# One split of x instead of three: an input projection in three sweeps, with the recurrences beside two of them

## The chip, the cores and the metric

The kernel runs on one core of one Trainium2 chip. A core has a matrix engine (PE; its weight loads are listed apart as PEld), a vector engine (DVE), a scalar engine (ACT), a general engine (POOL) and a sync engine (SP), which here does nothing but issue DMAs. The metric is the device time of one execution in microseconds; smaller is better. Three runs of the kernel before gave 3016.13, 3017.36 and 3020.99 us. All durations and waits are from one profiled execution of it.

## The reference

One encoder block on x of 2048 rows by 1024 columns, float32. The part that the change touches:

```python
h = rmsnorm(x, norm1_g)
p = h @ w_in                          # 1024 -> 1536: lru_x 512 | lru_gate 512 | fourier 512
c = centred_depthwise_conv(lru_x)     # width 4, along positions
h_f = rglru(c, ..., reverse=False)    # gates: 8 heads of 64x64 matmuls, sigmoid, then a linear
h_b = rglru(c, ..., reverse=True)     #   recurrence along the 2048 positions, in each direction
y_lru  = gelu(lru_gate) * (h_f + h_b)
y_four = real(fft2(fourier columns))  # per group of 128 channels
x = x + concat([y_lru, y_four]) @ w_out
x = x + expert_choice_moe(rmsnorm(x)) # 16 SwiGLU experts, 256 rows each
out = rmsnorm_final(x)
```

## The kernel before

**Matmuls.** Each float32 product is three matmuls in a reduced float32 format (`mm3`, L78 to L80): high part times high part, and the two mixed products. To have the parts, `split` copies a tile with rounding on ACT (the high part, L85 or with a row factor L88) and subtracts on DVE (the low part, L86 or L89). So whatever PE reads has first been through one ACT and one DVE (or POOL) instruction.

**Order.** The kernel is written in Tile, whose scheduler sets the order on each engine within dependencies; `soon()` raises the priority of what stands in it, and `tc.issue_after` holds an instruction behind another. Each engine then runs its instructions strictly in that order. Nearly all loads are issued from SP, also in one order: a DMA whose condition isn't met holds up all that stand behind it. POOL issues a few stores itself. A DMA also waits for one of eight lanes per kind of queue to be free (`DMAHW0` to `DMAHW7` in the lists below).

**Stages up to w_out**, all in `pre_moe`. Blocks are 128 columns; a chunk is 256 rows of x, a tile 128 rows.

- *First sweep*, `p1(0)`: columns of lru_x, blocks 0 and 1: 8 chunks of 48 matmuls of 256 columns. x comes as `xr` tiles of 128x512 and is split to `xx` (L197 ACT, L201 DVE or L199 POOL). The squares of x (L204, ACT) are added on POOL (`xa`, L239); `rms` sums them over the partitions by matmuls with a column of ones (L286), which gives one number per row, spread over partitions. Since the projection has rows along the free axis, `rstd` is stored to a buffer `r_d` in HBM and loaded back into all partitions as `R` (L222, SP). The evacuation (L254, DVE) multiplies the product by R into `u`.
- *Second sweep*, `p1(1)`: blocks 2 and 3, x loaded and split again; ahead of it stands `lru(0)`, the convolution (L328 POOL, L330 DVE), the split of its result c (`ch` L331, `cl` L332), the gates' matmuls (`gt<-ch,gm`, 48 of 512 columns), their sigmoids (L339), tanh, exp, square root, and two scans (L361, L363, DVE) of block 0.
- *Fourier sweep*: 16 tiles, 27 matmuls of 512 columns each (`mixin`, `stage1`), x loaded and split a third time (`load_xt`: L212 DVE, L213 POOL). `lru(1)`, `lru(2)` and `lru(3)` stand among the tiles. The first FFT stage's results `v` go to `v_d` in HBM by stores from POOL.
- *Gate sweep*: 8 chunks of 96 matmuls of 256 columns, x loaded and split a fourth time; per chunk DVE multiplies by R (`tm`, L435), ACT takes the Gelu (L438), DVE multiplies into `u` (L441).
- *FFT*: the second stage over positions and the channel stage, from `v_d` (`vraw`) and twiddles (`traw`); w_out is loaded and split meanwhile (`woraw`, L458 ACT, L459 POOL).
- *w_out*, routing and the experts follow.

Of the kernel before, what the change touches and what calls it, by code (L numbers as in the profile page):

```python
# [75 lines left out]
def mm3(nc, out, sh, sl, mh, ml, first=True, last=True, shared=False):  # L76
    """shared: groups of one bank are interleaved; the bank's first matmul alone starts it"""
    nc.tensor.matmul(out, sh, mh, start=first, stop=False, skip_group_check=shared)  # L78
    nc.tensor.matmul(out, sh, ml, start=False, stop=False, skip_group_check=shared)  # L79
    return nc.tensor.matmul(out, sl, mh, start=False, stop=last, skip_group_check=shared)  # L80
# [67 lines left out]
def pre_moe(tc, nc, a, g, ctx):  # L148
# [11 lines left out]
    last = {}  # L160

    for n, b in (("wraw", 2), ("w", 8), ("xraw", 4), ("xx", 6)):
        WP.tile([P, 512 * (1 + (n in ("w", "xx")))], F32R, name=n, bufs=b)

    def load_w(c0, n, k):
# [7 lines left out]
    def load_w2(c0, k2):
        """two k of a 256-column part"""
        with soon():
            if c0:
                raw = WP.tile([P, 2, 256], F32, name="wraw", bufs=2)
            else:
                raw = pr.tile([P, 2, 256], F32, name="wr1", bufs=8)
            nc.sync.dma_start(raw, a["w_u"][c0 // 256, k2])  # L180
            if c0:
                w = pl.tile([P, 2, 2, 256], F32R, name="fv"[k2 // 2], bufs=2)
            else:
                w = pr.tile([P, 2, 2, 256], F32R, name="w1", bufs=4)
            for i in range(2):
                split(nc, raw[:, i], w[:, 0, i], w[:, 1, i], g.g1[:, 2 * k2 + i:2 * k2 + i + 1])
        return [w[:, :, 0], w[:, :, 1]]

    def load_x(c, k2, pool=False, sq=None):
        with soon():  # L190
            if sq is not None:
                raw = pr.tile([P, 2, 256], F32, name="xr1", bufs=8)
            else:
                raw = WP.tile([P, 2, 256], F32, name="xraw", bufs=4)
            x = WP.tile([P, 2, 2, 256], F32R, name="xx", bufs=6)
            nc.sync.dma_start(raw, a["xT"][c, k2])
            last["ACT"] = nc.scalar.copy(x[:, 0], raw)  # L197
            if pool:
                GP.tensor_tensor(x[:, 1], raw, x[:, 0].bitcast(F32), OP.subtract)  # L199
            else:  # L200
                last["DVE"] = V.tensor_tensor(x[:, 1], raw, x[:, 0].bitcast(F32), OP.subtract)  # L201
# [4 lines left out]

    def load_xt(t, hf):
        with soon():
            raw = WP.tile([P, 4, P], F32, name="xraw", bufs=4)
# [2 lines left out]
            V.tensor_copy(x[:, 0], raw)  # L212
            GP.tensor_tensor(x[:, 1], raw, x[:, 0].bitcast(F32), OP.subtract)  # L213
# [5 lines left out]
    def load_R(c):  # L219
        R = WP.tile([P, 256], F32, name="R", bufs=2)  # L220
        src = g.r_d[c:c + 1]
        nc.sync.dma_start(R, bass.AP(tensor=src.tensor, offset=src.offset, ap=[[0, P], [1, 256]]))  # L222
        return R

    qbi = lambda x: x.rearrange("p (q b i) -> p q b i", q=2, b=16)

    def p1_load(h, c, w):
        xx = []
        acc = pr.tile([P, 2, 256], F32, name="xa", bufs=4) if h == 0 else None
        for k2 in range(4):  # L230
            if c == 0:
                w[2 * k2], w[2 * k2 + 1] = load_w2(256 * h, k2)
            if h:
                xx += load_x(c, k2, pool=k2 % 2 == 1)
                continue
            sq = pr.tile([P, 2, 256], F32, name="sq0", bufs=8) if k2 else acc
            xx += load_x(c, k2, sq=sq)
# [8 lines left out]

    def p1(h, w, pre):
        pend = []

        def evac(c, pt):  # L250
            R = load_R(c)
            with soon():
                for b in range(2):
                    V.tensor_tensor(u_view(2 * h + b, c), qbi(pt[:, b * 256:(b + 1) * 256]), qbi(R), OP.mult)  # L254
# [1001 lines left out]
```

## Time and profile before

| | |
|---|---|
| median of 3 runs | 3017.36 us (3016.13 to 3020.99) |
| span of the profiled execution | 3013.5 us, granted PE clock 0.969 |
| PE, weight loads, DVE, ACT, POOL busy in it | 2835.5, 2611.9, 1859.7, 1300.4, 559.6 us |
| first sweep | 0 to 95.3 us |
| second sweep | 95.3 to 180.6 us |
| fourier sweep | 180.6 to 371 us |
| gate sweep | 371 to 464 us |
| FFT | 464 to 517 us |
| w_out, the second norm, the router | 517 to 759 us |
| choice of rows, experts, final norm | 759 to 3013.5 us |

The profiled execution's span lies 3.9 us below the median of the runs; what surrounds it isn't in the profile. The stages' limits are read from the timeline of PE. In the profile a row of a group gives line, engine, operation, output and inputs with their shapes, the count, then busy us and mean ns of one, and behind the bar the idle time of the engine before them with what ended it. "PEclk" is the share of full clock granted to PE.

### The profile page before, as it was taken

Reading aid. Unit: us, or ns where it says so; the run is one execution under the profiler, and the core shown is the slowest. Engines: PE = TensorE matmul, PEld = TensorE weight load, DVE = VectorE, ACT = ScalarE, POOL = GpSimd, SP = SyncE. Lnnn points to the kernel's source line nnn. Section 1 sums busy time; section 2 is a strip of 40 time slices with the busy share of each in tenths; the row PEclk is TensorE's granted clock in tenths of the full one; section 3 lists DMA queues with packets and bytes.
Section 4 is the critical chain, followed back from the end, with each engine's and each line's share of the span. In section 5 each row is a group of like instructions: output and inputs, shape, how many; then the busy total and the mean of one; then the engine's idle time right before and its main releaser. Section 6 shows DMA issues by size and latency. Waiting matters only on the chain.

```text
span 3013.5 us, 45335 instructions
## 1 busy us (share of the span) xinstructions
PE 2835.5 (94%) x19199; PEld 2611.9 (87%) x19199; DVE 1859.7 (62%) x2146; ACT 1300.4 (43%) x1377; POOL 559.6 (19%) x412
## 2 busy tenths in 40 slices
PE   6677898996789999999999999999999999999997
PEld 6666697775679999999999999999999999999997
DVE  6588877556876555555665555555555655555565
ACT  5455654333234434343443444443434444343465
POOL 4375402002322111112021111111020111111110
PEclk8888999998889999999999999999999999999999
DMA  5532243454346565656656565656566565656585
GB/s 158 121 109 67 89 151 108 150 159 175 140 166 212 196 196 196 198 197 207 201 188 213 196 199 197 205 194 202 192 196 206 198 209 196 198 196 197 196 296 205
DMA packets 129196, 548.07 MB, mean 182 GB/s; under 512 B 20416, under 2 KB 37216, under 8 KB 79840
## 3 DMA queue, kind: packets, MB, share of 16 engines
q1 hardware_dynamic: 107664, 481.16, 47.3%
q0 software_dynamic: 19008, 63.98, 7.5%
q8 instruction: 150, 2.46, 0.3%
q14 instruction: 54, 0.44, 0.0%
q10 hardware_dynamic: 2320, 0.04, 0.0%
HBM read 498.97 MB, written 46.15 MB: 181 GB/s over the span
## 4 chain that ended last, share of the span: by engine, by line
PE 69%; DVE 3%; issue 2%; DMA 1%; POOL 0%; POOLq 0%; ACT 0%; DVEq 0%
PE mm L78 16%; PE mm L79 15%; PE mm L80 15%; PE dn L78 7%; PE dn L79 7%; PE dn L80 7%; DVE junk L833 1%; DVE wl L86 0%; DMA rows<-h_d,ix 0%; PE gt L969 0%; DMA rows<-h_d,iq 0%; DVE base L851 0%; DVE cq L836 0%; DVE cr L834 0%; DVE cs L835 0%
## 5 line engine op out<-in xcount | busy, mean ns | idle before, releaser
L86 DVE TENSOR_TENSOR wl<-raw,wh 128x2048 fp32r<-128x2048 f32 x374 | 868.4, 2326 | 564.5 <-ACT wh L85 563.6
L85 ACT CAST wh<-raw 128x2048 fp32r<-128x2048 f32 x374 | 711.2, 1906 | 1138.7 <-PE mm L79 764.2
L80 PE MATMUL mm<-xh,wl 128*128 128x256 f32 x4096 | 1163.1, 284 | 19.9 <-DVE wl L86 19.9
L78 PE MATMUL mm<-xh,wh 128*128 128x256 f32 x4096 | 1165.2, 284 | 0.0
L79 PE MATMUL mm<-xl,wh 128*128 128x256 f32 x4096 | 1163.7, 284 | 0.1
L80 PEld LDWEIGHTS mm<-xh,wl 128*128 128x128 f32 x4096 | 788.7, 193 | 21.0 <-DVE wl L86 20.9
L78 PEld LDWEIGHTS mm<-xh,wh 128*128 128x128 f32 x4096 | 788.6, 193 | 7.4 <-ACT xh L85 0.2
L79 PEld LDWEIGHTS mm<-xl,wh 128*128 128x128 f32 x4096 | 788.8, 193 | 5.7 <-DVE xl L86 0.4
L78 PE MATMUL dn<-wh,hh 128*128 128x512 f32 x1024 | 400.0, 391 | 0.0
L79 PE MATMUL dn<-wl,hh 128*128 128x512 f32 x1024 | 399.9, 391 | 0.0
L80 PE MATMUL dn<-wh,hh 128*128 128x512 f32 x1024 | 398.4, 389 | 0.0
L1110 POOL DMA_INDIRECT acc<-y,ix x30 | 60.0, 2001 | 1104.2 <-DVE y L1109 1020.0
L1010 POOL DMA_INDIRECT rows<-h_d,iq x120 | 139.6, 1164 | 592.5 <-DVE iq L991 560.5
L80 PEld LDWEIGHTS dn<-wh,hh 128*128 128x128 f32 x1024 | 192.3, 188 | 40.9
L78 PEld LDWEIGHTS dn<-wh,hh 128*128 128x128 f32 x1024 | 192.7, 188 | 36.7
L79 PEld LDWEIGHTS dn<-wl,hh 128*128 128x128 f32 x1024 | 192.7, 188 | 35.2
L1082 DVE TENSOR_TENSOR sg<-sg,mm 128x512 f32<-128x512 f32 x128 | 87.3, 682 | 152.9 <-PE mm L80 147.7
L1032 DVE STREAM_TRANSPOSE z<-rows 128x256 f32<-128x256 f32 x120 | 74.5, 656 | 129.1 <-DMA rows<-h_d,iq 121.3
L85 ACT CAST hh<-sg 128x512 fp32r<-128x512 f32 x128 | 78.7, 615 | 117.8 <-DVE sg L1082 117.6
L78 PE MATMUL mm<-woh,mh 128*128 128x512 f32 (+1 forms) x264 | 102.9, 390 | 0.8 <-ACT mh L85 0.8
L86 DVE TENSOR_TENSOR hh<-sg,hh 128x512 fp32r<-128x512 f32 x128 | 102.7, 803 | 0.7 <-ACT hh L85 0.7
L80 PE MATMUL mm<-woh,ml 128*128 128x512 f32 (+1 forms) x264 | 103.1, 391 | 0.0
(403 smaller groups left out, 3398.3 us busy)
## 6 DMA issues: line engine op xcount, KB each, us to landing
raw<-w_gate SPq DMA_DIRECT2D x128, 1024.0 KB, 4.9
raw<-w_up SPq DMA_DIRECT2D x128, 1024.0 KB, 4.8
raw<-w_down SPq DMA_DIRECT2D x128, 1024.0 KB, 5.0
xraw<-xT SPq DMA_DIRECT2D x96, 256.0 KB, 2.8
xr<-xT SPq DMA_DIRECT2D x32, 256.0 KB, 4.4
xrow<-x SPq DMA_DIRECT2D x16, 512.0 KB, 4.3
acc<-x POOLq DMA_DIRECT2D x16, 512.0 KB
h_d<-xrow POOLq DMA_DIRECT2D x16, 512.0 KB
```

Of the source, the lines that this page charges most:

```text
L78: nc.tensor.matmul(out, sh, mh, start=first, stop=False, skip_group_check=shared)
L79: nc.tensor.matmul(out, sh, ml, start=False, stop=False, skip_group_check=shared)
L80: return nc.tensor.matmul(out, sl, mh, start=False, stop=last, skip_group_check=shared)
L85: nc.scalar.copy(hi, raw)
L86: return nc.vector.tensor_tensor(lo, raw, hi.bitcast(F32), OP.subtract)
L833: V.scalar_tensor_tensor(junk, sc, dl, base.to_broadcast([P, 256]), op0=op, op1=OP.is_ge, accum_out=ct[:, 0:1])
L1010: nc.gpsimd.indirect_dma_start(out=r[:, o * 256:(o + 1) * 256], out_offset=None, in_=g.h_d.rearrange("t (q c) -> (t q) c", q=4), in_offset ...
L1032: V.transpose(out=xt[:, :, 32 * o:32 * o + 32], in_=comb(rows[o // 4][:, o % 4 * 256:(o % 4 + 1) * 256]))
L1082: turn[e, c] = V.tensor_tensor(sg, sg, pu, OP.mult)
L1110: nc.gpsimd.indirect_dma_start(out=g.acc, out_offset=bass.IndirectOffsetOnAxis(ap=idx[h][:, :1], axis=0), in_=y, in_offset=None, compute_o ...
```

## The change

x is split once. The first sweep now takes all four blocks of lru_x (96 matmuls a chunk), and SP stores each split tile, high and low part, to a new HBM buffer `x_d` (32 stores of 512 KB). The other two sweeps load the parts from there (`next_x`, L211), with no instruction on ACT, DVE or POOL. In `rms` a 128x128 matrix of ones makes the row sums in all partitions at once; the square root and a reciprocal of 128x256 give `R`, kept in 8 buffers; `r_d` is gone. The old column form of rstd stays, for the fourier sweep.

`lru(0)` and `lru(1)` stand at the start and in the middle of the fourier sweep, `lru(2)` and `lru(3)` at the start and in the middle of the gate sweep. In the gate sweep the product times R (`tm`) is stored from POOL to a new buffer `gt_d`; behind the sweep four loads `gl` of 1 MB bring it back by blocks, and Gelu and the product with `u` are done on 128x2048 tiles. In `lru` the first term of the convolution goes from POOL to ACT, c comes in halves, the split of c goes from a DVE copy and subtract of 1024 columns to ACT and DVE of 512, and the matmuls run over quarters of the positions first. Weights of the first sweep come through `load_w`, with two raw buffers where there were eight. From the first matmul of w_out on, every engine has the same instructions in the same order.

```diff
+    x_d = g.dr.tile([8, 4, P, 1024], F32, name="x_d")
+    gt_d = g.dr.tile([8, 2, P, 512], F32, name="gt_d")
...
+            if c == 0:
+                w[2 * k2], w[2 * k2 + 1] = load_w(0, 2 * k2), load_w(0, 2 * k2 + 1)
+            with soon():
+                raw = pr.tile([P, 2, 256], F32, name="xr", bufs=8)
+                x = WP.tile([P, 2, 2, 256], F32R, name="xx", bufs=6)
+                nc.sync.dma_start(raw, a["xT"][c, k2])
+                last["ACT"] = nc.scalar.copy(x[:, 0], raw)
                 last["DVE"] = V.tensor_tensor(x[:, 1], raw, x[:, 0].bitcast(F32), OP.subtract)
+                nc.sync.dma_start(x_d[c, k2], x.rearrange("p a b t -> p (a b t)").bitcast(F32))
...
+        for i in range(2):
+            nc.tensor.matmul(q[:, :256], ones_r, sp[:, i], start=i == 0, stop=i == 1)
...
+        nc.scalar.activation(R, q[:, :256], AF.Sqrt, scale=1.0 / D, bias=g.eps)
+        V.reciprocal(R, R)
-        nc.scalar.dma_start(g.r_d[c].rearrange("(h p) -> p h", p=P), r2)
...
+        def gates(c, w, xx):
+            pt = [ps.tile([P, 512], F32, name="mm", bufs=8 - g.ngt) for _ in range(2)]
+            four(pt, w, xx)
+            with soon():
+                for i in range(2):
+                    tm = pl.tile([P, 512], F32, name="v", bufs=4)
+                    V.tensor_tensor(tm..., pt[i]..., Rs[c][:, None, :].to_broadcast([P, 2, 256]), OP.mult)
+                    GP.dma_start(gt_d[c, i], tm)
...
+        for c in range(8):
+            if c in (0, 4):
+                load_gm(2 + c // 4)
+                lru(2 + c // 4)
+            if c + 1 < 8:
+                pre[c + 1] = next_x(c + 1)
+            gates(c, w, pre.pop(c))
         for b in range(4):
+            gl = pl.tile([P, S], F32, name=("rf", "if", "rb", "ib")[b], bufs=1)
+            nc.sync.dma_start(gl..., gt_d[:, b // 2, :, b % 2 * 256:b % 2 * 256 + 256]...)
+            with tc.issue_after(g.last_sqrt.ins):
+                nc.scalar.activation(gl, gl, AF.Gelu_apprx_tanh)
+            V.tensor_tensor(uv, uv, gl.rearrange("p (t b i) -> p t b i", t=16, i=8), OP.mult)
```

**SP in the first sweep.** Before, the loads of x (L196) alternate with the loads of R, each of which waits for the store of `rstd`:

```order
L222 DMA R<-r_d 128x256 [waits DMAHW6_49,DMAHW3_49]
L196 DMA xr_747<-xT 128x512 [waits DMAHW7_49,DVE_49,Activation_49]
L196 DMA xr_754<-xT 128x512 [waits DMAHW0_49,DVE_49,Activation_49]
L196 DMA xr_762<-xT 128x512 [waits DMAHW1_49,DVE_49,Activation_49]
L196 DMA xr_770<-xT 128x512 [waits DVE_49,Activation_49]
L222 DMA R<-r_d 128x256 [waits DMAHW4_49,DMAHW2_49]
```

Now the loads of x (L191) alternate with the stores of its parts (L194), each of which waits for DVE to have made the low part:

```order
L191 DMA xr<-xT 128x512 [waits DMAHW1_49]
L194 DMA x_d<-xx 128x1024 [waits DMAHW2_49,DVE_49]
L191 DMA xr<-xT 128x512 [waits DMAHW3_49]
L194 DMA x_d<-xx 128x1024 [waits DMAHW4_49,DVE_49]
L194 DMA x_d<-xx 128x1024 [waits DMAHW5_49,DVE_49]
L191 DMA xr<-xT 128x512 [waits DMAHW6_49]
L194 DMA x_d<-xx 128x1024 [waits DMAHW7_49,DVE_49]
L191 DMA xr<-xT 128x512 [waits DMAHW0_49]
```

The round trip of R has left this queue; a store of 512 KB behind each split has come into it, one to four loads behind the load of its own tile.

**DVE between the first and the fourier sweep.** Before, the splits of the second sweep's and the fourier sweep's weights stand among evacuations and splits of x (`xx`) in which one recurrence's convolution (`c`) is mixed:

```order
L89 SCALAR_TENSOR_TENSOR w<-wraw,vec,w 128x512 [waits DMAHW6_49,Activation_49]
L332 TENSOR_TENSOR cl<-c,ch 128x1024 [waits DVE_49]
L201 TENSOR_TENSOR xx<-xraw,xx 128x512 [waits DMAHW2_49,Activation_49]
L89 SCALAR_TENSOR_TENSOR w<-wraw,vec,w 128x512 [waits DMAHW1_49,Activation_49]
L341 TENSOR_TENSOR if<-if,c 128x2048 [waits Activation_49]
L89 SCALAR_TENSOR_TENSOR w<-wraw,vec,w 128x512 [waits DMAHW0_49,Activation_49]
```

Now the fourier sweep's weights (`w`) and block 0's convolution share this place:

```order
L86 TENSOR_TENSOR gm<-wraw,gm 128x512 [waits DMAHW5_49,DMAHW3_49,DMAHW6_49,DMAHW2_49,DMAHW1_49]
L290 SCALAR_TENSOR_TENSOR c<-u,vec,c 128x1024 [waits Activation_49]
L89 SCALAR_TENSOR_TENSOR w<-wraw,vec,w 128x512 [waits DMAHW6_49,Activation_49]
L290 SCALAR_TENSOR_TENSOR c<-u,vec,c 128x1024 [waits DVE_49]
L290 SCALAR_TENSOR_TENSOR c<-u,vec,c 128x1024
L89 SCALAR_TENSOR_TENSOR w<-wraw,vec,w 128x512 [waits DMAHW0_49,Activation_49]
L290 SCALAR_TENSOR_TENSOR c<-u,vec,c 128x1024 [waits DVE_49]
L89 SCALAR_TENSOR_TENSOR w<-wraw,vec,w 128x512 [waits DMAHW1_49,Activation_49]
```

The splits of x are gone from this stretch; the last five of the eight weight splits stand behind the start of the convolution, with a load through two raw buffers ahead of each.

**SP between the gate sweep and the FFT.** Before, the loads of the FFT's inputs stand among the gate sweep's own loads of x:

```order
L196 DMA xraw<-xT 128x512 [waits DMAHW6_49,DMAHW2_49,DVE_49]
L471 DMA traw<-tw 128x384 [waits PE_49]
L477 DMA vraw<-v_d 128x512 [waits DMASW4_49,DMASW5_49,DMASW3_49,DMASW6_49,DMASW2_49,DMASW7_49,DMASW1_49,DMASW0_49]
L477 DMA vraw<-v_d 128x512
L471 DMA traw<-tw 128x384
L222 DMA R<-r_d 128x256 [waits DMAHW7_49,DVE_49]
```

Now they stand behind all loads of w_out and the four loads of `gt_d`, which wait for stores of the last chunk (`DMASW` lanes):

```order
L390 DMA rf<-gt_d 128x8x256 [waits DMASW4_49,DMASW2_49,DMASW6_49,DMASW0_49,DMAHW7_49,DVE_49,Activation_49]
L410 DMA woraw<-w_out 128x1024 [waits DMAHW5_49,DMAHW0_49,Pool_49]
L410 DMA woraw<-w_out 128x1024 [waits DMAHW6_49,DMAHW1_49,Pool_49]
L390 DMA if<-gt_d 128x8x256 [waits DMAHW2_49]
L390 DMA rb<-gt_d 128x8x256 [waits DMASW5_49,DMASW7_49,DMASW3_49,DMAHW3_49,DMASW1_49,DVE_49]
L410 DMA woraw<-w_out 128x1024 [waits DMAHW4_49,DMAHW0_49,Pool_49]
L410 DMA woraw<-w_out 128x1024 [waits DMAHW1_49,Pool_49]
L390 DMA ib<-gt_d 128x8x256
L410 DMA woraw<-w_out 128x1024 [waits DMAHW7_49,DMAHW4_49,Pool_49]
L410 DMA woraw<-w_out 128x1024 [waits DMAHW5_49,Pool_49]
L424 DMA traw<-tw 128x384 [waits DMAHW3_49,DVE_49]
L430 DMA vraw<-v_d 128x512 [waits DMAHW2_49]
```

So the first load for the FFT has moved from the gate sweep's middle to behind six loads of w_out that wait for POOL (L459 in the kernel before) and the last of the four loads of `gt_d`.

More of the change, by code (lines that the diff above doesn't have):

```diff
@@ L158, in pre_moe @@
     WP = tc.alloc_tile_pool(name="WP", bufs=1, side="right", reuse_waits="tile")
[L160 to L165, printed above, removed]
+    for n, b in (("wraw", 2), ("w", 8), ("xx", 6)):
+        WP.tile([P, 512 * (1 + (n != "wraw"))], F32R, name=n, bufs=b)
+    WP.tile([P, 256], F32, name="R", bufs=8)
+    x_d = g.dr.tile([8, 4, P, 1024], F32, name="x_d")
+    gt_d = g.dr.tile([8, 2, P, 512], F32, name="gt_d")
@@ L171, in load_w @@
         return w
[L173 to L200, printed above, removed]
+    def u_view(b, c):
+        return u[:, b, 2:2 + S].rearrange("p (b t i) -> p t b i", t=16, i=8)[:, 2 * c:2 * c + 2]
@@ new lines, in pre_moe, with first_x @@
+    qbi = lambda x: x.rearrange("p (q b i) -> p q b i", q=2, b=16)
+    last = {}
+    Rs = {}
+    parts = lambda x: [(x[:, 0, i], x[:, 1, i]) for i in range(2)]
+    def first_x(c, w):
+        xx = []
+        acc = pr.tile([P, 2, 256], F32, name="xa", bufs=3)
+        for k2 in range(4):
+            if c == 0:
[5 more added lines that the diff above has]
+                last["ACT"] = nc.scalar.copy(x[:, 0], raw)
@@ L216, in u_view @@
-    def u_view(b, c):
-        return u[:, b, 2:2 + S].rearrange("p (b t i) -> p t b i", t=16, i=8)[:, 2 * c:2 * c + 2]
[L219 to L237, printed above, removed]
@@ L276, in pre_moe, with next_x, four @@
-    accs = {}
-    def rms(c):
-        acc = accs.pop(c)[0]
+        return xx, acc
+    def next_x(c):
+        xx = []
+        for k2 in range(4):
+            with soon():
+                x = WP.tile([P, 2, 2, 256], F32, name="xx", bufs=6)
+                nc.sync.dma_start(x.rearrange("p a b t -> p (a b t)"), x_d[c, k2])
+            xx += parts(x.bitcast(F32R))
+        return xx
+    def four(pt, w, xx):
+        for k in range(KD):
+            for b in range(4):
+                bs_ = slice(b * P, (b + 1) * P)
+                last["PE"] = mm3(nc, pt[b // 2][:, (b % 2) * 256:(b % 2) * 256 + 256], w[k][:, 0, bs_], w[k][:, 1, bs_], xx[k][0], xx[k][1],
+                                 k == 0 and b % 2 == 0, k == KD - 1 and b % 2 == 1, shared=True)
@@ L354, in lru @@
+            with tc.issue_after(x.ins):
                 for d in range(2):
```

207 lines of the change are left out of this document (79 added, 128 removed).

## The prediction

> **What bounds the kernel now.** I read the stages first, by busy time of each engine in windows cut where PE changes its work. Columns: window and its length, busy us and instructions of PE, weight loads, DVE, ACT, POOL, then granted PE clock, DMA share, GB/s.
>
> ```profile
> 0.00:95.30 95.30, 62.99 (x416) 60.79 (x416) 52.45 (x103) 49.38 (x97) 37.57 (x52) 0.86 0.56 137
> 95.30:180.60 85.30, 64.92 (x433) 60.76 (x433) 60.12 (x71) 47.08 (x69) 37.96 (x22) 0.86 0.54 133
> 180.60:371.00 190.40, 146.69 (x575) 115.55 (x574) 156.66 (x107) 106.19 (x119) 108.67 (x63) 0.89 0.27 81
> 371.00:464.00 93.00, 93.00 (x773) 92.84 (x773) 66.38 (x95) 46.65 (x62) 6.07 (x6) 1.00 0.45 141
> 464.00:517.00 53.00, 42.83 (x288) 39.32 (x286) 44.17 (x75) 32.29 (x62) 19.71 (x8) 0.90 0.34 111
> 517.00:759.00 242.00, 213.38 (x1050) 168.62 (x1050) 143.41 (x343) 85.03 (x177) 35.85 (x59) 0.93 0.48 158
> 759.00:3013.50 2254.50, 2211.70 (x15669) 2074.04 (x15669) 1336.49 (x1355) 933.77 (x796) 313.72 (x205) 0.99 0.59 200
> ```
>
> Behind 517 us nothing changes, on any engine, so the gain is the shift of that moment. Ahead of it only the gate sweep runs without a gap: 768 matmuls of 256 columns in 93.0 us, 0.121 us each. At this price the first two sweeps' 768 would take 93 us; they take 180.6. What stops PE there is in the waits (engine, line, what it waited for; us in total, times, longest), of SP and DVE in the first sweep and of PE up to 517 us:
>
> ```profile
> SPq L222 <- DMA r_d<-rstd: 34.5, 5, 13.1
> ...
> DVE u L254 <- DMA R<-r_d: 25.3, 4, 10.0
> ...
> PE gt L79 <- DVE cl L332: 20.3, 5, 10.5
> PE gt L286 <- DVE sp L86: 17.6, 5, 6.8
> PE gt L78 <- DVE ch L331: 17.5, 4, 6.3
> PE mm L78 <- ACT v L88: 10.5, 1, 10.5
> PE mm L79 <- DVE xx L201: 8.0, 2, 4.2
> ```
>
> SP stands 34.5 us before loads of R, with loads of x behind them; DVE stands 25.3 us for R, with splits behind it. So the first sweep is bound by the round trip of R, and the recurrences by the split of c. A tile-row of 512 columns costs PE, in a stretch of the fourier sweep without a gap:
>
> ```profile
> 234.33:246.90 12.57, 12.40 (x55) 9.97 (x54) 12.57 (x11) 12.54 (x12) 10.99 (x8) 1.00 0.28 83
> ```
>
> 12.57 us for 54 weight loads is 0.233 us a matmul.
>
> **The change, part by part.** The prices that I use, by groups (busy us, mean ns) and by tiles (min/median/max ns), then loads (KB, us to landing) and queues (packets, MB, share of the 16 engines) in 0 to 20 and 520 to 700 us:
>
> ```profile
> L213 POOL TENSOR_TENSOR xx<-xraw,xx 128x512 fp32r<-128x512 f32 x32 | 78.4, 2452 | 31.8 <-DVE xx L212 19.4 <-issue 11.6 <-POOL xx L213 0.4
> ...
> L197 ACT CAST xx<-xr 128x512 fp32r<-128x512 f32 x32 | 19.4, 615 | 18.1 <-PE mm L80 9.5 <-DMA xr<-xT 6.6 <-DMA pick<-cc 1.2
> ...
> L201 DVE TENSOR_TENSOR xx<-xr,xx 128x512 fp32r<-128x512 f32 x32 | 26.4, 845 | 6.6 <-ACT xx L197 6.6
> ...
> L88 ACT ACTIVATE w<-wraw,vec 128x512 fp32r<-128x512 f32 x16 | 11.3, 722 | 2.3 <-DMA wraw<-w_in 2.3
> ...
> L89 DVE SCALAR_TENSOR_TENSOR w<-wraw,vec,w 128x512 fp32r<-128x512 f32 x16 | 14.8, 941 | 2.8 <-ACT w L88 2.8
> ...
> L361 DVE TENSOR_TENSOR_SCAN u<-rf,if 128x2048 f32<-128x2048 f32 x4 | 17.9, 4479 | 0.0
> ...
> L435 DVE TENSOR_TENSOR tm<-mm,R 128x512 f32<-128x512 f32 x10 | 6.5, 686 | 6.6 <-PE mm L80 4.4 <-DMA R<-r_d 2.1
> ...
> L438 ACT ACTIVATE tm<-tm 128x1024 f32<-128x1024 f32 x8 | 8.4, 1057 | 21.7 <-DVE tm L435 21.6
> ...
> L459 POOL TENSOR_TENSOR wol<-woraw,woh 128x1024 fp32r<-128x1024 f32 x8 | 19.7, 2468 | 70.0 <-DVE xfl L86 57.8 <-ACT woh L458 12.1
> ...
> L458 ACT CAST woh<-woraw 128x1024 fp32r<-128x1024 f32 x8 | 8.5, 1059 | 1.2 <-DMA woraw<-w_out 1.1
> ```
>
> ```profile
> L330 DVE SCALAR_TENSOR_TENSOR c<-u,vec,c x24: 1251/1650/2320, 118.4 to 342.7; 128x1024 f32<-128x1024 f32 x24
> L332 DVE TENSOR_TENSOR cl<-c,ch x8: 1209/2053/7478, 133.3 to 347.3; 128x1024 fp32r<-128x1024 f32 x8
> ```
>
> ```profile
> xr<-xT SPq DMA_DIRECT2D x16, 256.0 KB, 4.4
> q1 hardware_dynamic: 3128, 5.70, 80.7%
> q0 software_dynamic: 3867, 14.14, 20.3%
> wraw<-w_in SPq DMA_DIRECT2D x4, 256.0 KB, 3.6
> woraw<-w_out SPq DMA_DIRECT2D x2, 512.0 KB, 4.7
> traw<-tw SPq DMA_DIRECT2D x6, 192.0 KB, 3.7
> ```
>
> *First sweep.* It starts PE at 6 us, as before. Its first chunk now waits for eight weights through two buffers: a pair takes 3.6 to land, 0.72 on ACT and 0.94 on DVE, 5.3 us; four pairs are 21 us, and with the last weight's matmuls the chunk ends near 30 us. It can't end before 6 + 96 x 0.121 = 18, nor, by twice the wait of a pair, much after 40. The seven others are 672 x 0.121 = 81.3. The row sums add two matmuls of 256 columns and four of 2 a chunk, at no more than 0.121 each, so some 0.6 us, 8 times: 4.8. Sum 116 us, against 180.6 for the same products and one recurrence before. The reciprocal, the evacuations and the splits of the next tiles run on DVE beside the 11.6 us of a chunk. The stores of x's parts, 16.8 MB, are costed at nothing: the loads run at 5.70 MB / (0.807 x 20 us) = 353 GB/s while busy, POOL's stores at 14.14 / (0.203 x 180) = 387, so a chunk needs 1.05 / 0.353 + 2.1 / 0.387 = 8.4 us of DMA under 11.6 of PE. Without that cover it is the third rival. Below nothing it can't go.
>
> *Fourier sweep.* 16 x 27 x 0.233 = 100.7, and two recurrences' matmuls 96 x 0.233 = 22.4. What stalls PE: at its start there is no work under the eight weights and block 0's convolution, which share DVE (3 x 1.65 for half of c, eight weights at 0.94): between 12 and 17 us; sigmoids that pace the gate matmuls, 3; `lru(1)`'s split behind the first one's scans, between 3 and 8 us; the last two tiles, 2. Together 24, and 147 for the sweep; it ends at 263. The 48 subtractions that POOL loses (L213 alone 78.4 us) and the 7.5 us longest `cl` are why I take less than before's stalls; the second rival takes those.
>
> *Gate sweep.* 93.0 as before, and 22.4 for two recurrences. Stalls: weights, whose loads now stand behind the fourier sweep, 4; `lru(3)`'s c behind `lru(2)`'s scans (4.48 and its like), 7.5; sigmoids, 4. Together 131; it ends at 394. Between nothing and the second rival's 37 for these stalls.
>
> *The join.* The four `gl` loads need the last chunk's stores. From its last matmul: evacuation 1.4 (two of 0.69, `tm`), store about 4 (the loads' 4.4), then 26 us in which SP issues `gl` and w_out's loads in turn: two pairs of w_out's tiles each wait 4.7 + 1.06 + 2 x 2.47 = 10.7 for the pair before, and two Gelus (2 x 1.06 each) stand between on ACT; then 3.7 for the twiddle and 2 for its split. That overlaps the last chunk by some 4: PE has nothing for about 33 us. The least is evacuation, store, one load and a Gelu ahead of the splits, 20; with w_out's three waits in full and no overlap 45. I take 33 since the order has all of w_out ahead of the twiddle. This is what the change gives back.
>
> *FFT.* 53.0 before; DVE and POOL no longer split w_out in it (POOL 19.7 us are done in the join), so I take 47, between PE's own 42.8 plus a start of 1 and 53. w_out starts at 394 + 33 + 47 = 474 instead of 517: 43 us earlier. Against the span of 3013.5, that gives 2970.5; the profiled execution lies 3.9 below the median of 3017.4, so 2974.
>
> **Rivals.** First, *all stalls shrink*. For it: POOL was busy 108.7 of the fourier sweep's 190 us, and `cl` took from 1.21 to 7.48 us for the same shape, so DVE's times beside an idle POOL would be the minima. Against it: waits on ACT and loads don't depend on POOL. Fourier and gate stalls at half are -20, the join at 28 and the FFT at 44 are -8: 2946. The Trainium skill ("SBUF — State Buffer", Who interferes with whom) says that a DVE instruction with two inputs in SBUF contends with a POOL instruction that reads SBUF, on ports that DVE shares with it. By that rule this rival would be the forecast; the rows of `cl` agree with it, but no run here shows yet what is left without POOL.
>
> Second, *each recurrence stops PE as now*. The fourier sweep held three; its work is 100.7 + 144 x 0.233 = 134.3 of 190.4 us, so 18.7 us of stall for each. Four are 75 where I have 39.5: +35, 3009. For it: scans, exps and tanhs are the same instructions, one recurrence waits for the one before. Against it: c's split is 512 wide and on two engines.
>
> Third, *the first sweep is bound by DMA*. The loads' queue in 520 to 700 us and in 20 to 95 us:
>
> ```profile
> q1 hardware_dynamic: 15391, 14.29, 29.1%
> ```
>
> ```profile
> q1 hardware_dynamic: 4472, 7.26, 46.8%
> ```
>
> 14.29 / (0.291 x 180) = 273 GB/s and 7.26 / (0.468 x 75) = 207 GB/s while busy. At 207 a chunk's 3.15 MB take 15.2 us, or with rows of 4 KB for the stores somewhat less: 7 x 3 = +21, 2995. Against it: small transfers are in that stretch.
>
> Fourth, on the other side, *the stores hold the loads*. SP issues in order, and a store that waits for DVE holds the next load, as L222's 34.5 us show for R. If no load got ahead, each of the 32 tiles would take 4.4 + 0.62 + 0.85 = 5.9 us one after the other: 6 + 188 = 194 us for the sweep where I have 116: +78, 3052, slower. It decides from (116 + 43 - 6) / 32 = 4.8 us a tile on. Against it: the order has one to four loads ahead of the store of their own time. The Trainium skill says that DMA engines do not wait on semaphores, and that the wait is the issuing engine's ahead of the transfer ("DMA: Bandwidth & Descriptors", Anatomy of one DMA). The wait of SP at L222 agrees; by this rule alone, without the loads issued ahead, the fourth rival's time would come out.
>
> **How the numbers follow.** Forecast 0.46, its own range 2958 to 2990 by the bounds of its stalls and the join; first rival 0.18, second 0.14, third 0.13, fourth 0.09. From 2944 to 3010 the first, the third and most of the second are in; the fourth, half of the second and the lower end of the first are out, 0.2. A measurement of this kernel can tell about 0.2% from no change: 6 us. Faster by more: 0.46 + 0.18 + 0.13 and 0.09 of the second, 0.86; within it 0.05, the rest of the second; slower 0.09.
>
> **What would show it.** R's 25 and 34 us are gone from the waits of DVE and SP, and the first sweep's last projection matmul ends near 116 us. If the third rival holds, chunks take 15 us there and the DMA share stands near 1; if the fourth, SP waits at L194 for DVE. The fourier sweep ends near 263 and the gate sweep, now with gaps, near 394. Then PE has nothing for some 33 us, with DVE or ACT waiting for the first twiddle. w_out's first matmul is near 474. If everything up to the gate sweep comes out and the whole doesn't, the join was mis-sized: each us there is a us of the result.

## The result: 72 us faster, and the profile after

The changed kernel takes 2944.4 us (2941.45 to 2945.96) against 3016.74 us in the runs beside it: ratio 0.9761, 95% interval 0.9748 to 0.9774. That is 72 us where 43 were forecast; the median lies 0.4 us inside the low end of the wide range (2944 to 3010) and outside the forecast's own (2958 to 2990). Its profiled execution has a span of 2942.2 us, 71.3 less than before. The windows of the changed kernel, cut again where PE changes its work (first sweep, fourier sweep, gate sweep, join, FFT, w_out to router, the rest):

```profile
0.00:110.50 110.50, 101.39 (x816) 100.28 (x816) 68.99 (x128) 52.19 (x99) 36.15 (x50) 1.00 0.80 284
110.50:244.20 133.70, 126.76 (x530) 100.99 (x530) 97.57 (x88) 96.90 (x119) 19.28 (x23) 0.96 0.48 164
244.20:369.25 125.05, 117.39 (x866) 110.20 (x865) 70.26 (x57) 70.62 (x77) 20.76 (x26) 1.00 0.51 176
369.25:402.50 33.25, 0.03 (x1) 0.03 (x1) 12.61 (x7) 16.31 (x15) 21.41 (x10) 0.57 0.80 264
402.50:449.10 46.60, 42.17 (x289) 38.53 (x289) 38.67 (x82) 28.21 (x61) 1.10 (x1) 0.94 0.36 110
449.10:687.70 238.60, 211.20 (x1014) 166.84 (x1014) 141.31 (x334) 85.05 (x177) 35.08 (x58) 0.94 0.49 160
687.70:2942.20 2254.50, 2214.19 (x15705) 2076.47 (x15705) 1339.81 (x1364) 932.74 (x796) 314.82 (x205) 0.99 0.59 200
```

The three sweeps now keep PE busy for 92 to 95% of their time; the fourth row is a stretch with no matmul at all. w_out starts at 449.1 us instead of 517.0, so 67.9 of the 71.3 us lie ahead of it. Not all of it is PE waiting less: the granted clock is 0.86 in both of the old kernel's first sweeps and 1.00 in the new one. The last section comes back to this. The waits of PE and of SP in the first 480 us of the changed kernel:

```profile
PE mm L78 <- ACT vl L85: 35.2, 5, 33.2
PE mm L78 <- ACT w L88: 6.5, 4, 2.9
PE gt L79 <- DVE ch L86: 6.4, 4, 2.9
PE mm L78 <- ACT xx L192: 6.3, 1, 6.3
PE gt L229 <- ACT sp L85: 1.9, 1, 1.9
...
SPq L194 <- DVE xx L193: 29.8, 22, 2.7
...
SPq L390 <- DMA gt_d<-v: 18.6, 2, 13.9
SPq L410 <- POOL wol L412: 17.6, 6, 6.1
```

The waits for the recurrence's split fell from 20.3 and 17.5 to 6.4 us, those for the row sums from 17.6 to 1.9. One wait of 33.2 us is new, for the FFT's first input. SP's queue in that join (start, us, line, DMA) shows why:

```profile
372.03 0.39 SPq L390 DMA_DIRECT2D rf<-gt_d  x1
373.21 2.62 SPq L410 DMA_DIRECT2D woraw<-w_out  x2
375.89 0.43 SPq L390 DMA_DIRECT2D if<-gt_d  x1
376.53 0.42 SPq L390 DMA_DIRECT2D rb<-gt_d  x1
385.12 2.65 SPq L410 DMA_DIRECT2D woraw<-w_out  x2
387.82 0.43 SPq L390 DMA_DIRECT2D ib<-gt_d  x1
393.98 2.63 SPq L410 DMA_DIRECT2D woraw<-w_out  x2
396.71 0.38 SPq L424 DMA_DIRECT2D traw<-tw  x1
```

The first twiddle is issued at 396.7 us, 27.5 us behind the last matmul, after gaps of 8.2 and 5.7 us ahead of pairs of w_out's loads, in which SP waits mostly for POOL.

### The profile page after: what moved, and what is told of

It is laid out like the page before. It is cut to its first block, busy times and chain, and to the rows that moved or that the text cites. A ratio compares the mean times of both kernels' runs of the same rounds, so it can differ in the third digit from the quotient of the medians.

```text
span 2942.2 us, 45045 instructions
## 1 busy us (share of the span) xinstructions
PE 2813.1 (96%) x19215; PEld 2593.3 (88%) x19215; DVE 1769.2 (60%) x2054; ACT 1282.0 (44%) x1341; POOL 448.6 (15%) x372
## 4 chain that ended last, share of the span: by engine, by line
PE 73%; DVE 3%; DMA 0%; issue 0%; POOLq 0%; ACT 0%; DVEq 0%
PE mm L78 16%; PE mm L79 16%; PE mm L80 16%; PE dn L78 8%; PE dn L79 8%; PE dn L80 8%; DVE junk L786 1%; PE gt L922 0%; DVE base L818 0%; DVE base L804 0%; DVE wl L86 0%; DMA rows<-h_d,ix 0%; DVE cq L789 0%; DVE cr L787 0%; DVE cs L788 0%
## 5 line engine op out<-in xcount | busy, mean ns | idle before, releaser
L1035 DVE TENSOR_TENSOR sg<-sg,mm 128x512 f32<-128x512 f32 x128 | 87.4, 683 | 152.9 <-PE mm L80 147.6
L78 PE MATMUL mm<-xx,w 128*128 128x256 f32 x512 | 146.2, 287 | 9.2 <-ACT xx L192 6.3
L79 PE MATMUL mm<-xx,w 128*128 128x256 f32 x512 | 145.1, 285 | 0.1
L80 PE MATMUL mm<-xx,w 128*128 128x256 f32 x512 | 144.2, 285 | 0.3 <-DVE w L89 0.3
```

Of the source, the lines that this page charges most:

```text
L1035: turn[e, c] = V.tensor_tensor(sg, sg, pu, OP.mult)
```

## The experiments

Where each kernel is at its stage boundaries, from PE's matmuls (us from the span's start; "ends" is the end of the gate sweep's last matmul); the median and the ratio are those of each kernel's runs against the kernel before.

| kernel | fourier sweep begins | gate sweep begins | ends | FFT begins | w_out begins | median | ratio, 95% interval |
|---|---|---|---|---|---|---|---|
| before | 180.5 | 371.1 | 464.0 | 463.8 | 517.0 | 3016.7 | 1 |
| after | 110.6 | 244.0 | 369.2 | 402.5 | 449.1 | 2944.4 | 0.9761 (0.9748 to 0.9774) |
| `r_alone` | 180.6 | 369.7 | 463.4 | 463.3 | 516.1 | 3012.7 | 0.9978 (0.9967 to 0.9989) |
| `split_again` | 118.9 | 275.9 | 400.1 | 426.0 | 486.6 | 2982.0 | 0.9883 (0.9855 to 0.9912) |
| `pool_busy` | 110.3 | 259.1 | 384.6 | 418.7 | 466.1 | 2961.5 | 0.9815 (0.9787 to 0.9844) |
| `w_out_later` | 110.5 | 243.3 | 370.4 | 390.2 | 453.5 | 2946.6 | 0.9766 (0.9738 to 0.9794) |
| `fft_first` | 112.3 | 243.9 | 371.1 | 373.4 | 437.7 | 2934.4 | 0.971 (0.9694 to 0.9726) |
| `stores_twice` | 148.9 | 284.9 | 410.9 | 444.3 | 491.5 | 2986.1 | 0.9884 (0.9865 to 0.9904) |
| `stores_by_pool` | 127.5 | 257.9 | 384.1 | 418.1 | 464.7 | 2964.7 | 0.9814 (0.9792 to 0.9835) |
| `gates_alone` | 111.7 | 263.0 | 376.3 | 380.0 | 438.0 | 2937.2 | 0.9723 (0.9707 to 0.9739) |
| `half_first` | 84.5 | 242.5 | 367.7 | 394.1 | 454.3 | 2949.2 | 0.9763 (0.9744 to 0.9783) |
| `r_by_hbm` | 169.9 | 317.5 | 443.4 | 477.5 | 528.4 | 3021.8 | 1.0004 (0.9994 to 1.0014) |
| `gates_direct` | 110.0 | 263.3 | 376.4 | 380.1 | 436.7 | 2935.7 | 0.9723 (0.9707 to 0.9739) |
| `direct_four` | 110.1 | 256.6 | 367.4 | 371.1 | 428.5 | 2928.0 | 0.9703 (0.969 to 0.9717) |

**R alone.** One part of the change put into the kernel before:

```diff
-            R = load_R(c)
+            R = load_R(c) if h else Rs.pop(c)
...
+        for i in range(2):
+            nc.tensor.matmul(q[:, :256], ones_r, sp[:, i], start=i == 0, stop=i == 1)
+        nc.scalar.activation(R, q[:, :256], AF.Sqrt, scale=1.0 / D, bias=g.eps)
+        V.reciprocal(R, R)
```

> The kernel before with one part of the change alone: in its first sweep R is made in all partitions by the 128x128 ones and used from there; the store to r_d stays and serves the later sweeps' loads. Theory (the round trip of R bound the first sweep): SP's 34.5 us and DVE's 25.3 us of waits go, and the first sweep's 95.3 us shrink by 20 to 25, to about 72; everything behind it keeps its length, so the whole comes to about 2992 to 2997. Rival (PE there was held by the order, by the row sums that wait for sp with 21.8 us, and by starting up): the waits of SP and DVE go, but the sweep keeps 88 to 95 us, the whole 3010 to 3017.

The rival held. DVE's 25.3 us of waits for R went, and the first sweep did not shrink at all: its last row sums end at 100.5 us instead of 95.1, the second sweep makes up for it, and w_out starts 0.9 us earlier. PE's waits in its first 95 us are the old ones:

```profile
PE gt L287 <- DVE sp L86: 15.2, 6, 7.8
PE mm L78 <- ACT xx L197: 6.0, 1, 6.0
PE gt L287 <- ACT sp L85: 5.7, 2, 4.7
PE mm L79 <- DVE xx L201: 3.5, 1, 3.5
```

So the reading "the first sweep is bound by the round trip of R" was wrong for the kernel before: the longest wait of a queue wasn't the one that ended last. One remainder: SP still waits 16.3 us at two loads of R for the second sweep that stand in this stretch (34.5 us at five before). That SP's waits with half of them gone leave the sweep as long speaks against them too, but they weren't all taken out.

**R by HBM in the new form.** The other way round, R's round trip put back into the changed kernel:

```diff
-        for i in range(2):
-            nc.tensor.matmul(q[:, :256], ones_r, sp[:, i], start=i == 0, stop=i == 1)
...
-        nc.scalar.activation(R, q[:, :256], AF.Sqrt, scale=1.0 / D, bias=g.eps)
...
-        V.reciprocal(R, R)
...
+        nc.scalar.dma_start(r_d[c].rearrange("(h p) -> p h", p=P), r2)
...
+        nc.sync.dma_start(R, bass.AP(tensor=src.tensor, offset=src.offset, ap=[[0, P], [1, 256]]))
```

> The changed kernel with R by the old way: rstd from the column form is stored from ACT's queue to HBM and loaded back into all partitions by SP, one load a chunk, ahead of the evacuation. Theory (with two banks of five a chunk, the evacuation of chunk c must come before chunk c + 2; the round trip of about 15 us is longer than a chunk of 12.2): PE waits 3 to 8 us in most chunks, the first sweep grows from 110.5 to 130 to 165, the whole 2964 to 3000. Rival (R's round trip is hidden here as its removal alone gained 0.2% in the kernel before): the sweep stays within 4 us, the whole under 2950.

It costs everything: the fourier sweep begins at 169.9 us instead of 110.6 and takes 147.6 instead of 133.4, and the whole is no faster than before, ratio 1.0004. The first sweep and the whole lie above the theory's ranges. Waits of PE and DVE in its first 169.9 us:

```profile
PE mm L78 <- DVE u L252: 41.6, 4, 26.0
...
DVE u L252 <- DMA R<-r_d: 55.0, 4, 22.3
```

PE now waits for the evacuation, once 26.0 us and then 4.9, 4.8 and 5.9: with four blocks a chunk takes two of five banks, and chunk c + 2 can't start before chunk c is evacuated. The waits expected "in most chunks" came in four; the long one comes from the first three loads of R, which SP issues together at 72.4 us, behind stores and a run of seven loads of x. The same part is worth 0.9 us at w_out's start in the old form and 79 in the new one.

**Two blocks a tile.** What then made the old sweeps slow was tried on the kernel of `split_again` (next), since there the stores are out of the way:

```diff
-            four(pt, w, xx)
+            two(pt, w, xx)
```

> The kernel that splits x again (no x_d), whose first sweep projects blocks 0 and 1 only: 48 matmuls a chunk instead of 96, the same tiles of x, squares and row sums; blocks 2 and 3 of lru_x are left out and zero. Theory (a sweep of two blocks is bound by making the tiles and the row sums in a circle of waits, and four blocks a tile hide it): the chunks behind the first don't come down to PE's 48 x 0.121 + 0.4 = 6.2 us but stay at 8 to 11 us, as in the kernel before (10.2), and the sweep ends at 80 to 100 us against 119 with four blocks. Rival (the old first sweep was slow through R's round trip and its order alone): chunks of 6.2 to 7 us, the sweep ends at 62 to 70 us.

The sweep ends at 80.9 us, as the theory had it. Counted by PE, each 48 matmuls behind the first 48 take 9.2 us (15.6 to 80.3 us); counted so, the kernel before takes 11.4 (14.3 to 94.3). In the sweep

```profile
0.00:80.90 80.90, 61.37 (x432) 58.84 (x432) 71.71 (x110) 50.63 (x99) 42.48 (x51) 0.94 0.48 154
```

DVE is busy 71.7 of 80.9 us and PE 61.4: what DVE does for a chunk takes longer than the 48 matmuls. The second 48 matmuls of each chunk, 46 us of PE in all, lengthen the sweep by 34 only (`split_again`'s last ends at 114). That explains part of why one sweep of four blocks beats two of two. The old sweep's 11.4 us with DVE busy 52 of 95 us is not explained by DVE's load; what else in its order cost 2 us a chunk wasn't taken apart.

**x split again.**

```diff
-                nc.sync.dma_start(x_d[c, k2], x.rearrange("p a b t -> p (a b t)").bitcast(F32))
...
+                nc.sync.dma_start(raw, a["xT"][c, k2])
+                if pool:
+                    V.tensor_copy(x[:, 0], raw)
+                    GP.tensor_tensor(x[:, 1], raw, x[:, 0].bitcast(F32), OP.subtract)
+                else:
+                    nc.scalar.copy(x[:, 0], raw)
+                    V.tensor_tensor(x[:, 1], raw, x[:, 0].bitcast(F32), OP.subtract)
```

> The changed kernel without x_d: the parts aren't stored, and the fourier sweep (DVE copy, POOL subtraction, as before) and the gate sweep (ACT copy, DVE subtraction) load x and split it again. Theory (parts kept in HBM are worth what the splits stall): the first sweep keeps its 110.5 us, as the stores were hidden; the fourier sweep grows from 133.7 to about 145 to 155 by 32 copies and subtractions and by POOL's slowing of DVE, the gate sweep from 125 to 127 to 132; the whole 2958 to 2975. Rival (ACT, DVE and POOL have room, R and the order did it all): no sweep changes by over 3 us, the whole 2940 to 2948.

w_out starts at 486.6 us, 37.5 later than with x_d and 30.4 earlier than before. Its fourier sweep and its gate sweep:

```profile
118.90:275.00 156.10, 133.58 (x524) 102.91 (x525) 141.59 (x116) 95.67 (x117) 82.71 (x55) 0.91 0.33 98
275.00:400.40 125.40, 118.96 (x870) 112.25 (x868) 84.68 (x85) 83.84 (x102) 16.93 (x23) 0.99 0.31 97
```

The theory held for the fourier sweep in kind: it grows by 22 us, to just above the range, and DVE is busy 141.6 of 156 us, 44 more than with x_d. It failed for the other two sweeps, and the whole (2982.0) lies above its range. In the gate sweep the split comes back on ACT and DVE, 13 and 14 us, and costs nothing: 125.4 against 125.05. The fourier sweep begins 8 us later: 4 of them are lost in the first sweep, where PE waits 5.1 us for a weight of the first chunk, and 4.3 are a wait for ACT, which is at block 0's convolution, ahead of the fourier sweep. So what the stored parts buy is 22 to 24 us in the sweep where POOL and DVE split and up to 8 ahead of it, none in the gate sweep; the last 7 come from the join and the FFT, in which w_out's loads fell elsewhere.

**POOL kept busy.** 32 subtractions of 128x512 that nothing reads, none of the rest changed:

```diff
+                if k in (0, 4):
...
+                    with tc.issue_after(last["PE"].ins):
+                        GP.tensor_tensor(scr, g.cc[:, 0:512], g.cc[:, 256:768], OP.subtract)
```

> The changed kernel with 32 extra POOL subtractions of 128x512 from a constant into a scratch tile in the fourier sweep, two per tile of 128 rows, as many as the kernel before had there; nothing reads them. Theory of the first rival (POOL slowed DVE, and its leaving is why the stalls shrank): the convolution's DVE instructions go back from 1.28 to a median of 1.6 or more, the low part of c from 0.69 to 1 to 2 us, and the fourier sweep grows from 133.7 by 6 to 12 us; the whole 2950 to 2957. Rival (DVE has slack now, its times are off the path): DVE's instructions stretch but the sweep grows by under 2 us. Third case: DVE's instructions don't stretch.

The scheduler didn't spread them: they ran from 94.5 to 149.8 us, where the fourier sweep starts. Of that stretch, this kernel's window first, then the changed kernel's, behind them the weights' DVE splits (min/median/max ns), again of this kernel and of the changed one, and PE's longest wait in this kernel's fourier sweep:

```profile
94.50:147.60 53.10, 39.75 (x214) 32.17 (x213) 45.21 (x37) 20.21 (x32) 50.76 (x33) 0.87 0.45 144
```

```profile
94.50:147.60 53.10, 49.12 (x268) 40.82 (x267) 36.62 (x46) 31.79 (x46) 1.60 (x3) 0.97 0.46 157
```

```profile
L89 DVE SCALAR_TENSOR_TENSOR w<-wraw,vec,w x8: 914/1744/1773, 100.6 to 138.5; 128x512 fp32r<-128x512 f32 x8
```

```profile
L89 DVE SCALAR_TENSOR_TENSOR w<-wraw,vec,w x8: 653/749/752, 100.8 to 128.0; 128x512 fp32r<-128x512 f32 x8
```

```profile
PE mm L79 <- DVE w L89: 8.3, 3, 3.2
```

The same split takes 1744 ns beside POOL and 749 without, 37 DVE instructions take 45 us where 46 took 37, PE waits 8.3 us for the weights' low parts where it had no such wait, and the gate sweep begins 15 us later, above the 6 to 12 expected. The first rival's mechanism is shown, at the place where PE needs what DVE makes next. The convolution's median over the sweep did not move (1286 against 1282 ns); its instructions inside the stretch mostly took 2.29 to 2.32 us. DVE's products with one input in PSUM, `u<-mm,R` and `f<-mm,rstd,f`, took 0.41 and 0.74 us there, as in the changed kernel: the instructions that stretched have both inputs in SBUF. The Trainium skill ("SBUF — State Buffer", Who interferes with whom) has a DVE instruction with two inputs in SBUF contend with a POOL instruction that reads SBUF; the 1744 and 749 ns agree.

**The stores: twice, and from POOL.**

```diff
+                nc.sync.dma_start(x_d2[c, k2], x.rearrange("p a b t -> p (a b t)").bitcast(F32))
```

> The changed kernel with each x_d store issued twice, the second to another buffer: 5.25 MB a chunk instead of 3.15. Theory (the stores were hidden with a cover of about 1.1 to 1.4): at the 297 to 353 GB/s seen a chunk then takes 15 to 17.7 us instead of 12.2, the first sweep grows from 110.5 by 20 to 40, the whole 2964 to 2984. Rival (the DMA engines have room for twice the stores at 420 GB/s): at most 5 us more, the whole under 2950.

The first sweep's last matmul ends 32.2 us later and the fourier sweep begins 38.3 us later, as the theory had it, and the whole grows to 2 us above its range. In the stretch from 20 to 148 us the packets of the loads' queue, which has the stores too, take 85.2% of the 16 DMA engines' time:

```profile
q1 hardware_dynamic: 13394, 40.91, 85.2%
```

40.91 MB / (0.852 x 128) = 375 GB/s while busy. The changed kernel's first sweep stands at a share of 0.80 already, so the stores are hidden by a thin cover. What binds with twice the stores is not settled: ACT waits 22.1 us for x to land (4.4 us in the changed kernel), but SP also stands 47.9 us at the stores for DVE's splits and evacuations (36.4 us in the changed kernel), with loads of x behind them. It can be the DMA engines or SP's order.

```diff
-                nc.sync.dma_start(x_d[c, k2], ...)
+                GP.dma_start(x_d[c, k2], ...)
```

> The changed kernel with the x_d stores issued from POOL's queue instead of SP's. Theory (SP's 29.8 us of waits for DVE at the stores held no load long enough to matter): SP's waits at the stores go and the first sweep stays at 110.5 within 2 us, the whole 2942 to 2948. Rival (the stores hold the loads somewhat, as the fourth rival had it): the first sweep gains 3 us or more.

Both theories fail: the sweep ends 17 us later. POOL's waits in its first 125 us:

```profile
POOL x_d L194 <- DVE xx L193: 38.2, 17, 10.6
POOL xa L199 <- ACT sq L197: 15.1, 8, 5.8
```

The wait for DVE has only changed queues. On SP it held loads that were issued far enough ahead; on POOL it stands ahead of the sums of squares, which make the row sums late and hold the raw tiles of x that the squares read. PE's longest wait behind its start is 4.7 us for `sp`, whose low part took DVE 5.28 us once instead of 0.43 (min/median/max ns):

```profile
L86 DVE TENSOR_TENSOR sp<-xa,sp x8: 396/426/5283, 45.0 to 112.7; 128x256 fp32r<-128x256 f32 x8
```

It ran from 44.95 to 50.23 us, beside four POOL additions that stood behind a store and ran without a gap from 45.0 to 49.9. About 11 of the 17 us are PE standing still (20.4 us in the sweep against 9); in the rest it works at a lower granted clock, 0.79 from 20 to 60 us where the changed kernel has 1.00. How much comes from POOL's own issuing wasn't separated.

**The join.** The FFT's inputs were given memory that the gates' tiles don't use, their first loads a higher priority, and w_out's loads were put behind them:

```diff
+    for n_, sh_, dt_, b_ in (("cs", ...), ("xfh", ...), ("xfl", ...), ("bs", ...), ("traw", ...), ("tw", ...), ("vraw", ...), ("vl", ...)):
+        pf.tile(sh_, dt_, name=n_, bufs=b_)
...
-        with soon():
+        with soon(), tc.issue_after(last["v", 0].ins):
             nc.sync.dma_start(raw, a["w_out"][k * P:(k + 1) * P])
...
-        with soon():
+        with soon() if i else tc.high_priority(offset=4 * g.soon):
```

> The changed kernel with the loads of w_out put behind the first loads of the FFT's inputs, whose tiles lie in memory that the gl tiles don't use; the gl loads, Gelu and products stay ahead. Theory (the join is SP's queue, held by w_out's three waits for POOL): the 33.3 us without PE shrink to 18 to 24, the FFT goes from 46.6 back to 50 to 54 since w_out is split in it again, the whole 2934 to 2941. Rival (the join is the return of the gates, DMA of 4.2 MB and Gelu): it keeps 28 us or more, the whole 2944 to 2952.

The join shrinks to 19.8 us, as the theory had it, and the FFT grows from 46.6 to 63.3, beyond it: 4.4 us lost at w_out's start. Its two windows, and the splits of the FFT's inputs on DVE in this kernel and in the changed one:

```profile
370.50:390.20 19.70, 0.02 (x1) 0.02 (x1) 8.59 (x5) 10.12 (x9) 1.10 (x2) 0.62 0.86 286
390.20:453.50 63.30, 49.32 (x288) 45.20 (x288) 50.72 (x82) 35.46 (x69) 19.22 (x8) 0.82 0.45 147
```

```profile
L86 DVE TENSOR_TENSOR vl<-vraw,vl x16: 676/688/2817, 392.0 to 443.2; 128x512 fp32r<-128x512 f32 x16
```

```profile
L86 DVE TENSOR_TENSOR vl<-vraw,vl x16: 677/692/694, 404.3 to 438.5; 128x512 fp32r<-128x512 f32 x16
```

82 DVE instructions of the FFT take 50.7 us beside POOL's subtractions for w_out and 38.7 without. The 33 us were not idle: POOL split w_out in them, where PE waited for nothing that DVE had still to make. With the first FFT inputs ahead of the gates' return too, which comes in half blocks into the weights' memory:

```diff
-            gl = pl.tile([P, S], F32, name=("rf", "if", "rb", "ib")[b], bufs=1)
+            gl = WP.tile([P, 2, 512], F32R, name="w", bufs=8)...
...
             x = stage2(i, gr)
+            if i == 0:
+                gate_back(gr)
```

> The changed kernel with the first FFT loads ahead of the gates' return: the gl tiles lie in the weights' memory in eight halves, their loads, Gelu and products stand among the first FFT set's matmuls, and w_out's loads behind them. Theory (the join is nothing but what was put ahead of the first twiddle): PE is without work for 5 to 10 us instead of 33.3, the FFT takes 47 to 56, the whole 2918 to 2932. Rival (DVE and ACT then bound the FFT, with 38.7 + 12.6 and 28.2 + 16.3 us of work in it): the FFT grows by what the join loses, to 65 or more, the whole 2938 to 2946.

PE is without work for 2.3 us only, and the FFT takes 64.3, so w_out starts 11.4 us earlier than in the changed kernel. The result lies between the theory's and the rival's: the join gives 30.9 us and the FFT takes back 17.7 and the sweeps 1.9.

**Recurrences beside the fourier sweep alone.**

```diff
-            if c == 4:
-                load_gm(1)
-                lru(1)
+            if c in (2, 4, 6):
+                load_gm(c // 2)
+                lru(c // 2)
...
-            if c in (0, 4):
-                load_gm(2 + c // 4)
-                lru(2 + c // 4)
...
-                    GP.dma_start(gt_d[c, i], tm)
+                    with tc.issue_after(g.last_sqrt.ins):
+                        nc.scalar.activation(tm, tm, AF.Gelu_apprx_tanh)
```

In `gates_alone` the product with the gates is made for blocks 2 and 3 only.

> The changed kernel with one part undone: all four recurrences stand in the fourier sweep, and the gate sweep has Gelu and product per chunk, with no gt_d and no return. Theory (ACT bounds a fourier sweep with four recurrences, 143 us of them and 26 of its own): it grows from 133.7 to 175 to 195, the gate sweep takes 93 to 97, PE is without work for 3 to 10 us behind it; the sum up to the FFT is 380 to 405 against 402.5, the whole 2920 to 2946. Rival (recurrences beside the gate sweep are where the gain is): the sum is above 415, the whole above 2955.

> The kernel of gates_alone with the product of the gates for all four blocks (gates_alone has it for blocks 2 and 3 alone): all four recurrences in the fourier sweep's program, Gelu and product per chunk, no gt_d. 16 products more of 0.42 us on DVE in a sweep in which DVE has room: theory, w_out starts at 437 to 442 us as in gates_alone (438.0), the whole 2935 to 2942, so placing the recurrences beside the gate sweep is worth nothing once it needs the return. Rival (the products come behind the last chunk): 443 or later, the whole 2943 or more.

With all products w_out starts at 436.7 us, 12.4 earlier than in the changed kernel. ACT did not bound the fourier sweep at 175 us as expected: the scheduler let the last recurrence run on into the gate sweep (its last gate matmul ends at 304.6 us, the gate sweep begins at 263.3), and the two sweeps together take 266.4 us against 258.6. But there is no return from HBM, the join is 3.7 us instead of 33.2, and the FFT takes 56.6. So `gt_d` is not where the gain is; the recurrences cost about the same in either place.

**Four raw buffers for the weights** in that kernel:

```diff
-            raw = WP.tile([P, 512], F32, name="wraw", bufs=2)
+            raw = WP.tile([P, 512], F32, name="wraw", bufs=4)
```

> The kernel of gates_direct with four raw buffers for the weights instead of two, in all three sweeps. Theory (the loads through two buffers are what PE still waits for at the starts of the sweeps: 7.9 us behind ACT's and 3.5 us behind DVE's splits of w in gates_direct): of these 11.4 us 4 to 9 go, w_out starts at 428 to 433 us instead of 436.7, the whole 2927 to 2932. Rival (the splits themselves, 1.7 us a weight on ACT and DVE beside the convolution, set the pace, not the buffers): w_out within 2 us of 436.7, the whole 2933 to 2938.

The theory held: w_out at 428.5 us, the whole 2928.0, the fastest of all, 16 us below the changed kernel. None of it comes in the first sweep, which ends at 110.1 us instead of 110.0; the two later sweeps give 6.7 and 2.4 us, and the FFT takes 0.8 back. PE's waits for the weights, first in `gates_direct`, then here:

```profile
PE mm L78 <- ACT w L88: 7.9, 8, 3.0
...
PE mm L80 <- DVE w L89: 3.0, 4, 1.4
```

```profile
PE mm L80 <- DVE w L89: 1.2, 2, 0.9
...
PE mm L78 <- ACT w L88: 0.9, 1, 0.9
```

## Why the prediction was right in sign and short in size

| term | predicted | measured |
|---|---|---|
| first sweep ends | 116 (first chunk 30) | 110.5 (first chunk 29) |
| fourier sweep | 147, with 24 of stalls | 133.4, with 10 |
| gate sweep | 131, with 15.5 of stalls | 125.2, with 10 |
| join | 33 | 33.2 |
| FFT | 47 | 46.6 |
| w_out starts | 474 | 449.1 |
| behind it | 0 | -3.4 |

- **The three work terms** (81.3 us for seven chunks, 123.1 and 115.4 us for the sweeps) came out: the chunks run at 12.2 us to the end, and what isn't PE's work is now 10 us in either sweep.
- **The stalls were mis-sized**, 20 us of the 28 that the forecast's span is short. The largest is the fourier sweep's start, where 12 to 17 us stood for weights and convolution with "no work under" them. PE stood still for 4.0 us there (24.50 less 20.52):

```profile
110.50:135.00 24.50, 20.52 (x79) 14.74 (x79) 21.96 (x28) 17.30 (x26) 0.53 (x1) 0.93 0.54 179
```

  So the overlap was wrong: two of the eight weights were split before the sweep began (by 101.6 and 107.0 us), and the first tiles' matmuls ran between the others. The prices were too high as well, but that is the smaller part: DVE's 0.94 (a mean) and 1.65 (a median) beside a busy POOL are 0.75 and 1.28 without it, 2.6 us of the 12.5 that they add up to. That the overlap rests on short DVE times is what `pool_busy` shows: with POOL's work at this place the 15 us come back. In the gate sweep PE waits 3.5 us for c's split where 7.5 stood, and not at all for the sigmoids, where 4 stood.
- **The first rival** had the number (2946) at a chance of 0.18, and that is in part luck. Its stalls at half came (20 of 39.5 us); its 8 us from a shorter join and FFT did not, and the first sweep's 5.5 and the 3.4 us at the end of the program, which it doesn't name, stand in their place. The wide range, which reaches down to 2944, holds the result by 0.4 us: that it came out inside is luck as much as forecast.
- **The first chunk** ended where the forecast had it. The last weight's low part was begun at 27.8 us, and the first evacuation, at 29.39, came 0.27 us behind what it waited for, PE:

```profile
L89 DVE SCALAR_TENSOR_TENSOR w<-wraw,vec,w x8: 652/748/752, 5.8 to 27.8; 128x512 fp32r<-128x512 f32 x8
```

```profile
29.39 1.42 DVE L252 TENSOR_TENSOR u<-mm,R 128x256 f32<-128x256 f32 x4 [0.27 <-PE mm L80]
```

  What failed is again the overlap: the sum has seven chunks behind the first, but PE ran the next chunk's matmuls while it was short of weights (96 were done at 23.8 us), and so the sweep ended 5.5 us earlier. With four buffers the eighth weight is ready at 21.2 us and the sweep ends no earlier (`direct_four`): the buffers matter at the later sweeps alone, 8.2 us at w_out's start.
- **What bounds the kernel now** was read wrongly: R's round trip as the first sweep's bound (`r_alone`: 0.2%). It would have become one in the new form (`r_by_hbm`), so this part had to come with the others. The gain that the text gave to it comes in part from four blocks on each tile (`half_first`); what else slowed the old sweeps is open.
- **The join** came out to 0.2 us, and its mechanism, SP's order, too (`w_out_later`). The sentence that each us there is a us of the result was wrong: `w_out_later` took 13.4 us from it and lost 4.4 in sum.
- **The third and fourth rival** did not come. There is a cover for the stores, but a thin one, of DMA or of SP's order (`stores_twice`). SP does wait 29.8 us for DVE at the stores, with no wait of PE behind the first chunk for x. **The second** did not come: the waits for the recurrences' split fell to 6.4 us.
- **Behind w_out**, 3.4 us shorter with the same instructions, and PE has no part in it: from w_out's first matmul to the last expert's it takes 2481.3 us in both kernels. From there to the end it is 15.3 us before and 11.8 after. `gates_direct` and `direct_four` take 15.3 there too, `pool_busy` and `w_out_later` 11.6, so it doesn't go with the change alone; what decides it is open.

## What to carry to other kernels

Before waits are added up in series, look for work of the next chunk or tile that the engine can do under them: here that was most of the error. Price a stage with the durations that its instructions will have beside their new neighbours, not with means taken beside the old ones: here the minima in the trace came nearest. A long wait of a queue proves a bound only if the work behind it is what ends last; put the fix in alone, and into the full change, before giving it the gain. An idle stretch of the main engine may be the place where another stage's work got done undisturbed, so price what moves out of it in the place where it goes.

## What the hardware showed that was not expected

POOL subtractions whose results nothing reads made the same DVE instruction 2.3 times as long (749 to 1744 ns median). Single ones took four times as long (0.69 to 2.8 us beside the subtractions for w_out) and once twelve times (0.43 to 5.28 us beside four POOL additions in a row). The same 512 KB stores cost no wait of PE that the trace shows from SP's queue and 17 us from POOL's.

In the sweeps where PE waits, its matmuls ran slower as well. In the old kernel's first two sweeps 133 matmuls of 256 columns followed one another at about 0.21 us instead of 0.12, in stretches where the granted clock was one half, some 50 us in all. One of them, with 16 matmuls in 3.4 us:

```profile
24.30:27.70 3.40, 3.40 (x16) 3.40 (x17) 3.19 (x12) 0.80 (x2) 0.00 (x0) 0.50 0.63 180
```

At 0.09 us each that is an estimate of 12 us of the gain. Behind its first 12 us the changed kernel's first sweep has no such stretch. The forecast had this gain in its price of 0.121 us without naming it. Why the clock is lowered there no run here shows.
